# First vectors loaded whole, RWKV's gate applied beside the last two chunks, the rotary key's low part in full-height tiles

## The chip, the cores and the metric

The kernel runs on one core of a Trainium2 chip. The metric is the device time of one execution in microseconds (us). The engines are named as the profile names them: PE (matrix multiplication; PEld is its weight load), DVE (vector), ACT (scalar), POOL (GpSimd) and SP (which issues most of the DMAs).

## What is computed

Two blocks follow each other on one sequence of 512 tokens of width 1024. The first is a two-layer network: layer 0 is an RWKV-7 time mix and a squared-ReLU MLP, layer 1 forgetting attention and an MLP. The second is a gated-DeltaNet mixer beside a latent attention (MLA), and then a layer of 16 experts. All is fp32 in and out. What the three edits touch, cut from the reference:

```python
# modulation of layer 0; sh1 and sc1 are needed first
mod = c_act @ mod_w[0] + mod_b[0]              # 1024 x 6144
sh1, sc1, gt1, sh2, sc2, gt2 = split(mod, 6)
h = rms_norm(x, g) * (1.0 + sc1) + sh1
# RWKV time mix
xx = token_shift(h) - h
xr, xw, xk, xv, xa, xg = (h + xx * mu[j] for j in range(6))
w_log = -softplus(-(w0 + tanh(xw @ w1) @ w2)) - 0.5
a = sigmoid(a0 + (xa @ a1) @ a2)
g = sigmoid(xg @ g1) @ g2                      # 1024 -> 160 -> 1024
... # r, k, v, then the scan over 512 tokens gives y, normalised per head
y = y * ln_w + ln_b + bonus
x = x + (1 + gt1) * ((y * g) @ wo)
# MLA scores: q and k have 128 plain and 64 rotary dimensions, the rotary key is shared by the 8 heads
s = q_nope @ k_nope.T + q_rope @ k_rope.T
```

## The kernel before

Activations lie transposed: eight tiles of 128 channels by 512 tokens. They come from one pool of 58 slots (`self.s()`), in the mixer from a second pool of 23 (also `self.s()`). A large matrix product is made of three products of rounded fp32 parts (fp32r): each operand is split into a high part, made on ACT, and a low part, made on DVE or POOL (`split`, `wsplit`, lines 168 to 206). Small products are plain fp32, and each of those shows in the trace as two passes on PE.

A planner (the Tile framework) orders each engine's instructions at build time, by a priority that grows with the place in the program and by its own estimates of when inputs are ready. On the chip every engine, and the SP queue too, then works strictly in that order. `behind(n)` lowers the priority of what is traced in it by n places. `issue_after(i)` puts what is traced in it behind instruction i on i's engine. A tile whose memory or slot is still in use makes the instruction that would fill it wait, and everything queued behind that.

**The start.** `load_x` (L2438) loads x. `mod_gen` (L319) then makes the two vectors that are needed first, the scale (v = 1) and then the shift (v = 0). Each is c (1 x 1024) times a 1024 x 1024 piece of `mod_w`, loaded as eight chunks of 256 rows by 512 columns into four buffers (`mr`, L327). The products are made in 32 of PE's columns, one row block for each quarter (L341), and then transposed on DVE (L344), summed on PE (L347) and added to the bias (L350). `rwkv` (L515) follows: the norm (`rstd_fm`), t = x times gain times rstd (L525, DVE), h = t + shift (L527, ACT), the token difference d (L529 from t, and its first column from h, L530, both POOL), and the six mixtures h + d mu (`mix`, L538, DVE). The low-rank products come next: w and a (L548, L549, in 64 columns each), then g's 1024 to 160 as one matmul of 128 columns (L560) and one of 32 (L561) for each of eight k. Their weights (`lw`) use the two `wr` buffers of the weight pool, which `rw_wv`'s tiles need next (L178). The value product begins at L271 (`dense_tm`).

**The scan.** Eight chunks of 64 tokens (L902 to L963). A chunk's chain is L920 (state and inputs), L934 (inverse), L945 and L948 (the next state); L952 makes its outputs, and `finish` (L833) normalises two chunks' outputs on DVE and ACT. Beside chunks 4 to 7 run `gates` (g's second product, eight steps) and `boni` (the bonus, eight steps, whose first step of each half fetches four tiles of v). How many steps a chunk gets stands in `GA_` and `GB_`, and they are put 150 places behind. Output tiles 0 and 1 (of 128 tokens) go to DRAM in between (`keep`).

**After the scan.** L969 to L990: the first weights of `rw_wo` are loaded and split on ACT and POOL, tiles 0 and 1 are fetched, and for each of eight channel blocks four 128 x 128 transposes (L985) bring y back to channels by tokens; DVE applies ln_w and the gate (L987), adds the bonus (L988), and the result z is split (ACT, then POOL or DVE). Then the product with `rw_wo` (L1001).

**The MLA scores.** `mla_gen` (L1822) runs between the DeltaNet's steps. Of a head's query rotary part, 64 rows of a tile hold the high part and the other 64 the low part (L1907 to L1909). The rotary key has its high part in both halves. Five matmuls make one 128 x 512 block of scores (L1922 to L1926), of which the last is the query's high part with the key's low part and reads 64 rows only:

```python
nc.tensor.matmul(pS, a[:, dq], kr[0][0], start=False, stop=False)
nc.tensor.matmul(pS, a[q, dq], kr[0][1][q], start=False, stop=True)
```

## Time and profile before

| | us |
|---|---|
| three runs | 2990.75, 2989.43, 2976.11 |
| median | 2989.43 |
| the profiled execution | 2976.45 |
| its span, first to last instruction | 2974.6 |

1.9 us of the profiled execution lie outside its span. The three runs fall on two levels, 2976 and 2990, and the profiled execution is on the lower one.

The page gives busy time by engine over the whole span. The stretches that matter here are 0 to 82 us (the start, to the first value matmul), 395 to 500 us (the scan's second half, and what follows it), 2235 to 2357 us (the MLA scores) and 2440 us to the end (the experts). In the timeline a line is: start, length, engine, line of the kernel, operation, tile written and tile read, shapes, count, and in brackets how long the engine was idle before it and what it waited for. A matmul's length is modelled and overlaps the next one; the step from start to start is the pace.

### The profile page before, as it was taken

To read this page: it belongs to the slowest core of one execution; us is meant where nothing else is said; L and a number is where in the kernel's file an instruction comes from. 1 tells how busy PE (TensorE), PEld (TensorE's weight loads), DVE (VectorE), ACT (ScalarE), POOL (GpSimd) and SP (SyncE) were. 2 spreads that over 40 slices of the span, in tenths; PEclk is the share of its full clock that TensorE was granted. 3 is DMA by queue.
4 is the path that set the end of the run, shared out by engine and by line. 5 is a ranking of instruction groups with operands and counts; after the bars stand their busy time and mean duration, and the time that the engine had idled before them with its cause. 6 is when DMAs were issued, how large, how long until landed. Compare 5 with 4: busy or idle time off the path is not lost.

```text
span 2974.6 us, 38010 instructions
## 1 busy us (share of the span) xinstructions
PE 2771.8 (93%) x15078; PEld 1976.9 (66%) x15078; DVE 1560.9 (52%) x2339; ACT 1057.5 (36%) x1692; POOL 708.1 (24%) x551
## 2 busy tenths in 40 slices
PE   5998888999999999999999997988989998999997
PEld 1665666788876777788886785866867784444333
DVE  4568755555673457565636776628535542212113
ACT  2555433422234467432223452344335432110001
POOL 2446533210110043111112432233252121000000
PEclk9998678999999999999999997999999999999999
DMA  6334215356572321455522322252162377999997
GB/s 211 121 89 143 86 60 177 99 170 198 187 241 78 96 66 45 135 187 194 170 86 71 100 75 76 58 162 57 62 196 91 100 234 293 406 403 409 409 409 299
DMA packets 361010, 502.06 MB, mean 169 GB/s; under 512 B 24768, under 2 KB 236992, under 8 KB 360832
## 3 DMA queue, kind: packets, MB, share of 16 engines
q1 hardware_dynamic: 349600, 479.01, 47.3%
q10 hardware_dynamic: 11232, 20.62, 1.9%
q8 instruction: 119, 1.95, 0.3%
q14 instruction: 59, 0.48, 0.0%
HBM read 471.26 MB, written 26.21 MB: 167 GB/s over the span
## 4 chain that ended last, share of the span: by engine, by line
PE 73%; DVE 13%; DMA 7%; issue 3%; ACT 3%; POOL 1%; SPq 1%; ACTq 0%; DVEq 0%; POOLq 0%
PE psb L243 11%; PE psb L245 11%; PE psb L244 11%; PE psb L2166 6%; PE psf L1322 5%; PE psb L1322 3%; PE psb L2206 3%; DMA rg<-in_w_down_dram 2%; DMA rg<-in_w_up_dram 1%; PE psb L1223 1%; DVE R L1401 1%; DVE s L1491 1%; PE psm L341 1%; PE psm L1957 1%; DVE tm L1399 1%
## 5 line engine op out<-in xcount | busy, mean ns | idle before, releaser
L243 PE MATMUL psb<-s,wh 128*128 128x512 f32 x1384 | 542.9, 393 | 3.1 <-DVE s L987 2.4
L244 PE MATMUL psb<-s,wl 128*128 128x512 f32 x1384 | 540.4, 390 | 0.0
L245 PE MATMUL psb<-s,wh 128*128 128x512 f32 (+1 forms) x1320 | 514.9, 390 | 1.2 <-POOL s L480 0.6
L180 ACT ACTIVATE wh<-wr 128x1024 fp32r<-128x1024 f32 (+1 forms) x221 | 288.2, 1305 | 423.1 <-PE psb L245 250.6
L182 DVE TENSOR_TENSOR wl<-wr,wh 128x1024 fp32r<-128x1024 f32 (+1 forms) x145 | 260.8, 1800 | 261.7 <-ACT wh L180 260.3
L243 PEld LDWEIGHTS psb<-s,wh 128*128 128x128 f32 x1384 | 259.6, 188 | 71.0 <-issue 11.4
L244 PEld LDWEIGHTS psb<-s,wl 128*128 128x128 f32 x1384 | 259.7, 188 | 56.4 <-issue 2.2
L245 PEld LDWEIGHTS psb<-s,wh 128*128 128x128 f32 (+1 forms) x1320 | 247.5, 188 | 57.8 <-issue 2.9
L182 POOL TENSOR_TENSOR wl<-wr,wh 128x1024 fp32r<-128x1024 f32 (+1 forms) x76 | 185.1, 2436 | 411.9 <-ACT wh L180 391.1
L2166 PE MATMUL psb<-rg,s 128*64 128x512 f32 x1024 | 254.8, 599 | 6.3 <-DMA rg<-in_w_up_dram 5.7
L1322 PE MATMUL psf<-f,wh 128*128 128x512 f32 (+1 forms) x688 | 236.6, 416 | 3.0 <-DVE f L1491 2.8
L1018 POOL TENSOR_TENSOR s<-s 128x512 f32<-128x512 f32 x64 | 102.2, 1597 | 514.9 <-ACT s L1016 434.1
L2166 PEld LDWEIGHTS psb<-rg,s 128*64 128x64 f32 x1024 | 83.9, 136 | 148.2 <-issue 125.1
L1322 PEld LDWEIGHTS psf<-f,wh 128*128 128x128 f32 (+1 forms) x688 | 131.8, 195 | 31.0 <-issue 4.5
L1322 PE MATMUL psf<-f,wl 128*128 128x512 f32 (+1 forms) x344 | 142.9, 415 | 3.4 <-POOL wl L182 3.3
L2206 PE MATMUL psb<-rg,s 128*64 128x512 f32 (+1 forms) x544 | 131.8, 573 | 7.4 <-DMA rg<-in_w_down_dram 7.2
L377 DVE SCALAR_TENSOR_TENSOR mt<-mr,crep,mt 128x512 f32<-128x512 f32 x168 | 126.5, 753 | 3.6
L200 ACT ACTIVATE s<-s 128x512 fp32r<-128x512 f32 x112 | 69.7, 625 | 137.4 <-POOL s L1018 73.1
L1322 PE MATMUL psb<-f,wh 128*128 128x512 f32 (+1 forms) x336 | 106.7, 397 | 7.8 <-DVE f L478 5.9
L1025 DVE SCALAR_TENSOR_TENSOR s<-psb,aff,s 128x512 f32<-128x512 f32 x64 | 45.9, 751 | 129.2 <-PE psb L245 129.2
L2206 PEld LDWEIGHTS psb<-rg,s 128*64 128x64 f32 x544 | 45.8, 136 | 80.6 <-issue 58.4
L2214 DVE SCALAR_TENSOR_TENSOR s<-psb,gate,s 128x512 fp32r<-128x512 f32 (+1 forms) x17 | 12.1, 719 | 164.3 <-ACT s L2213 163.9
(579 smaller groups left out, 4895.1 us busy)
## 6 DMA issues: line engine op xcount, KB each, us to landing
rg<-in_w_gate_dram SPq DMA_DIRECT2D x64, 1024.0 KB
rg<-in_w_up_dram SPq DMA_DIRECT2D x64, 1024.0 KB
rg<-in_w_down_dram SPq DMA_DIRECT2D x64, 1024.0 KB
mr<-in_mod_w_dram SPq DMA_DIRECT2D x96, 512.0 KB
wr<-in_mlp_down_dram SPq DMA_DIRECT2D x32, 1024.0 KB
wr<-in_mlp_up_dram SPq DMA_DIRECT2D x31, 1024.0 KB
wr<-in_w_in_dram SPq DMA_DIRECT2D x54, 512.0 KB
mr<-in_w_mod_dram SPq DMA_DIRECT2D x40, 512.0 KB
```

Source lines behind the costliest of these rows:

```text
L180: nc.scalar.activation(hi, raw, AF.Copy)
L182: (lo_eng or self.lo_eng or nc.vector).tensor_tensor(lo, raw, hi.bitcast(F32), op=OP.subtract)
L200: nc.scalar.activation(hi, src, AF.Copy)
L243: nc.tensor.matmul(pt[:mw], hi[k][:, j:j + mw], a, start=(k == 0), stop=False)
L244: nc.tensor.matmul(pt[:mw], lo[k][:, j:j + mw], a, start=False, stop=False)
L245: nc.tensor.matmul(pt[:mw], hi[k][:, j:j + mw], b, start=False, stop=(k == nk - 1))
L377: nc.vector.scalar_tensor_tensor(acc[:, hb], raw[:, d], c, acc[:, hb], op0=OP.mult, op1=OP.add)
L1018: nc.gpsimd.tensor_tensor(sq, r, r, op=OP.mult)
L1025: nc.vector.scalar_tensor_tensor(xT[m], pt, gt[:, m:m + 1], xT[m], op0=OP.mult, op1=OP.add)
L1322: nc.tensor.matmul(pt[:rows, :cols], x, y, start=(k == 0 and q == 0), stop=(k == nk - 1 and q == 2))
L2166: nc.tensor.matmul(B[n][q], XE[hp][k0 // 2][:, o:o + 64], w[e][:, k, n * 512:n * 512 + 512], start=(k0 + k == 0), stop=(k0 + k == 7), skip ...
L2206: last = nc.tensor.matmul(pt[q, :n], HT[(k + i) // 4][:, o:o + 64], w[e][i], start=(k + i == 0), stop=(k + i == 7), skip_group_check=True)
```

## The change

Three edits that do not depend on each other.

1. **Start.** The first two vectors come through a new `mod_first`: the sixteen chunks are 128 rows by all 1024 columns, each in a buffer of its own (16 of 4 KB a partition, in a pool that is closed before `rwkv` opens its own in the same memory). All sixteen loads are traced first. Each chunk gives two matmuls in the same 32 columns, one for each half of the outputs. Between the first vector and the second one's transposes, the norm, all eight t and all eight d (all but its first column) are traced; `issue_after` holds the transposes behind the last t on DVE. The low-rank weights leave the `wr` buffers and share one tile in the pool of `GB`. g's small matmuls go four at a time into four quarters of PE's columns and are summed by one more matmul.
2. **Scan.** The bonus steps are 3, 3, 2, 0 in chunks 4 to 7 where they were 2, 2, 2, 2. A new generator `outs` transposes output tiles 0 to 2 and applies the gate and the bonus to 384 columns, four channel blocks beside chunk 6 and four beside chunk 7, also 150 places behind. After the scan only the last 128 columns are left. The low part of z is made on DVE for four of eight blocks where it was two.
3. **MLA.** The rotary key's low part is kept twice, each in a full tile whose other half is zero, and the fifth matmul reads all 128 rows. One more slot of the 23 is held during the attention.

```diff
-GB_ = (0, 0, 0, 0, 2, 2, 2, 2)
+GB_ = (0, 0, 0, 0, 3, 3, 2, 0)
+MB = 16
...
+    def mod_first(self, jobs, pool):
+        nc = self.nc
+        raws = []
+        for _, W, v, _, _ in jobs:
+            for k in range(KT):
+                raw = pool.tile([128, D], F32, name=self.nm("mw"), tag="mw")
+                nc.sync.dma_start(raw, W[k * 128:k * 128 + 128, v * D:v * D + D])
+                raws.append(raw)
+        after = None
+        for cn, _, _, bias, out in jobs:
+            pts = [self.ps(), self.ps()]
+            for k in range(KT):
+                raw, q = raws.pop(0), slice(32 * (k % 4), 32 * (k % 4) + 32)
+                for hb, pt in enumerate(pts):
+                    nc.tensor.matmul(pt[q], self.crep[cn][:, k], raw[:, hb * 512:hb * 512 + 512], start=(k < 4),
+                                     stop=(k > 3), skip_group_check=True)
+            po = self.bank("m")
+            for hb, pt in enumerate(pts):
+                tp = self.s()
+                with self.tc.issue_after(after) if after else contextlib.nullcontext():
+                    nc.vector.transpose(tp, pt)
+                nc.tensor.matmul(po[:, hb * 16:hb * 16 + 16], self.cst("modsel"), tp[:, 0:512:32], start=(hb == 0),
+                                 stop=(hb == 1), skip_group_check=True)
...
+            after = yield
...
-        wa = self.wp.tile([128, KT, 128], F32, name=self.nm("lw"), tag="wr")
+        lw = gb0.tile([128, 32, 128], F32, name=self.nm("lw"), tag="gb", bufs=1).rearrange("p a b -> p (a b)")
+        wa = lw[:, 0:1024].rearrange("p (k n) -> p k n", n=128)
+        wg = lw[:, 1024:2304].rearrange("p (k n) -> p k n", n=160)
...
-        for k in range(KT):
-            if k % 4 == 0:
-                wg4 = self.wp.tile([128, 4, 160], F32, name=self.nm("lw"), tag="wr")
...
-            xg = mix(5, k)
-            nc.tensor.matmul(pg1, wg[:, 0:128], xg, start=(k == 0), stop=(k == 7))
-            nc.tensor.matmul(pg2[0:32], wg[:, 128:160], xg, start=(k == 0), stop=(k == 7))
+        for kb in (0, 4):
+            xg = [mix(5, kb + j) for j in range(4)]
+            for j in range(4):
+                nc.tensor.matmul(pg1, wg[:, kb + j, 0:128], xg[j], start=(kb + j == 0), stop=(kb + j == 7))
+            for j in range(4):
+                nc.tensor.matmul(pg2[32 * j:32 * j + 32], wg[:, kb + j, 128:160], xg[j], start=(kb == 0), stop=(kb == 4),
+                                 skip_group_check=True)
...
+        nc.scalar.activation(t, pg2, AF.Copy)
+        pg2 = self.ps()
+        nc.tensor.matmul(pg2[0:32], self.cst("modsel")[:, 0:32], t, start=True, stop=True)
...
+            def outs():
+                for g in range(2):
+                    yy = [self.fetch(Y[tt][g]) for tt in range(2)] + [Y[2][g]]
+                    for j in range(4):
+                        fs = slice(j * 128, j * 128 + 128)
+                        pa = self.ps()
+                        for tt in range(3):
+                            nc.tensor.transpose(pa[:, tt * 128:tt * 128 + 128], yy[tt][:, fs], idn)
+                        G, H = (x[:, 0:384] for x in GH[4 * g + j])
+                        nc.vector.scalar_tensor_tensor(G, pa[:, 0:384], self.col("rw_lnw", 4 * g + j), G, op0=OP.mult, op1=OP.mult)
+                        nc.vector.tensor_tensor(G, G, H, op=OP.add)
+                    del yy
+                    yield
...
                         step(GA_[c], GB_[c])
+                        if c > 5:
+                            next(ot2)
...
-            pa = self.ps()
-            for tt in range(4):
-                nc.tensor.transpose(pa[:, tt * 128:tt * 128 + 128], Y[tt][g][:, o:o + 128], idn)
+            if o == 0:
+                pa = self.ps()
+                for j in range(0, 512, 128):
+                    nc.tensor.transpose(pa[:, j:j + 128], Y[3][p // 4][:, j:j + 128], idn)
             G, H = GH[p]
-            nc.vector.scalar_tensor_tensor(G, pa, self.col("rw_lnw", p), G, op0=OP.mult, op1=OP.mult)
-            nc.vector.tensor_tensor(G, G, H, op=OP.add)
-            z.append(self.split(G, lo_eng=nc.gpsimd if p % 4 else nc.vector))
+            v = G[:, 384:512]
+            nc.vector.scalar_tensor_tensor(v, pa[:, o:o + 128], self.col("rw_lnw", p), v, op0=OP.mult, op1=OP.mult)
+            nc.vector.tensor_tensor(v, v, H[:, 384:512], op=OP.add)
+            z.append(self.split(G, lo_eng=nc.gpsimd if p % 2 else nc.vector))
...
-                kr[0] = self.split(kr[0])
+                hi = self.s(F32R)
+                nc.scalar.activation(hi, kr[0], AF.Copy)
+                lows = []
+                for b in (0, 64):
+                    lo = self.s(F32R)
+                    nc.gpsimd.memset(lo[64 - b:128 - b].bitcast(F32), 0.0)
+                    nc.vector.tensor_tensor(lo[b:b + 64], kr[0][b:b + 64], hi[b:b + 64].bitcast(F32), op=OP.subtract)
+                    lows.append(lo)
+                kr[0] = hi, lows
...
-            nc.tensor.matmul(pS, a[q, dq], kr[0][1][q], start=False, stop=True)
+            nc.tensor.matmul(pS, a[:, dq], kr[0][1][h % 2], start=False, stop=True)
...
-            self.run(self.mod_gen(self.mods("c", A["mod_w"][0], m0, (1, 0), M0)))
+            m0m = tc.tile_pool(name="m0", bufs=MB, side="right", reuse_waits="tile")
+            first = self.mod_first(self.mods("c", A["mod_w"][0], m0, (1, 0), M0), m0m.__enter__())
+            next(first)
             G = self.gain(col("norm_mix_g", 0, 8), M0[:, 1])
+            rstd = self.rstd_fm(xT)
+            ts = []
+            for k in range(KT):
+                t = self.s()
+                after = nc.vector.scalar_tensor_tensor(t, xT[k], G[:, k:k + 1], rstd, op0=OP.mult, op1=OP.mult)
+                d = self.s()
+                nc.gpsimd.tensor_tensor(d[:, 1:], t[:, :511], t[:, 1:], op=OP.subtract)
+                ts.append((t, d))
+                xT[k] = None
+            first.send(after.ins)
+            m0m.__exit__(None, None, None)
```

## Rows read from the trace of the kernel before

**Rows 1.** The page, part 1: PE's busy time, share of the span, instructions.

```profile
PE 2771.8 (93%) x15078; PEld 1976.9 (66%) x15078; DVE 1560.9 (52%) x2339; ACT 1057.5 (36%) x1692; POOL 708.1 (24%) x551
```

**Rows 2.** DMA view of 0 to 60 us: GB/s in forty slices of 1.5 us.

```profile
GB/s 0 174 409 397 400 393 377 378 397 388 277 53 294 388 395 384 360 352 344 242 123 356 337 326 323 307 286 200 238 249 354 382 180 49 15 0 0 11 0 0
```

**Rows 3.** Timeline of the start, PE: g's first products, the first value matmul.

```profile
64.39 1.13 PE L560 MATMUL psb<-s,lw 128*128 128x512 f32 x2
...
66.42 1.12 PE L560 MATMUL psb<-s,lw 128*128 128x512 f32 x2
...
81.99 0.51 PE L271 MATMUL psb<-wh,s 128*128 128x512 f32 x1 [1.28 <-ACT s L200]
```

**Rows 4.** Timeline of the start, DVE.

```profile
40.59 0.72 DVE L344 STREAM_TRANSPOSE mt<-psm 128x512 f32<-128x512 f32 x1 [8.23 <-PE psm L341]
41.82 0.69 DVE L350 TENSOR_TENSOR M<-psm,P 32x8 f32<-32x8 f32 x4 [0.51 <-PE psm L347]
42.54 6.29 DVE L525 SCALAR_TENSOR_TENSOR s<-s,gain,s 128x512 f32<-128x512 f32 x7
48.75 19.89 DVE L538 SCALAR_TENSOR_TENSOR s<-s,P,s 128x512 f32<-128x512 f32 x24
...
78.11 2.73 DVE L538 SCALAR_TENSOR_TENSOR s<-s,P,s 128x512 f32<-128x512 f32 x4
```

**Rows 5.** Groups of 0 to 82 us by form, ACT and POOL: h and d.

```profile
L529 POOL TENSOR_TENSOR s<-s 128x511 f32<-128x511 f32 x8 | 11.7, 1465 | 16.1 <-DVE s L525 16.1
L527 ACT ACTIVATE s<-s,M 128x512 f32<-128x512 f32 x8 | 5.5, 722 | 22.1 <-DVE M L350 20.6 <-DVE s L525 1.4
L530 POOL TENSOR_SCALAR s<-s 128x1 f32<-128x1 f32 x8 | 5.2, 647 | 13.7 <-ACT s L527 13.7
```

**Rows 6.** Timeline at 2462 us, PE: four column quarters, two matmuls in each.

```profile
2462.41 1.08 PE L2009 MATMUL psb<-s,s 128*32 128x512 f32 x8
2463.29 1.06 PE L2010 MATMUL psb<-s,s 128*32 128x512 f32 x8
```

**Rows 7.** Stretches of the scan's end: length, busy times, PEclk, DMA share, GB/s.

```profile
434.20:455.10 20.90, 19.53 (x179) 12.71 (x178) 7.28 (x13) 5.07 (x9) 8.94 (x9) 0.67 0.24 73
425.70:434.20 8.50, 8.50 (x151) 6.64 (x150) 3.15 (x6) 2.37 (x4) 2.08 (x3) 1.00 0.03 5
```

**Rows 8.** Timeline after the scan, PE: transposes, first matmul of rw_wo.

```profile
476.16 5.81 PE L985 MATMUL psb<-C,s 128*128 128x128 f32 x28 [4.98 <-DMA s<-kd]
...
486.86 0.77 PE L243 MATMUL psb<-s,wh 128*128 128x512 f32 x1 [2.36 <-DVE s L987]
```

**Rows 9.** Timeline of the SP queue, scan's end (merged: a length holds its waits).

```profile
433.17 18.24 SPq L1265 DMA_DIRECT2D s<-kd  x4
```

**Rows 10.** Groups of 470 to 500 us: DVE's two steps for z, POOL's weight split.

```profile
L988 DVE TENSOR_TENSOR s<-s,s 128x512 f32<-128x512 f32 x8 | 9.6, 1225 | 0.0
...
L182 POOL TENSOR_TENSOR wl<-wr,wh 128x1024 fp32r<-128x1024 f32 (+1 forms) x2 | 6.9, 3442 | 16.9 <-ACT wh L180 16.9
...
L987 DVE SCALAR_TENSOR_TENSOR s<-psb,P,s 128x512 f32<-128x512 f32 x8 | 5.7, 738 | 0.9 <-PE psb L985 0.9
```

**Rows 11.** Timeline of one MLA unit, PE.

```profile
2258.23 0.40 PE L1924 MATMUL psf<-f,f 128*128 128x512 f32 x1
2258.46 0.40 PE L1925 MATMUL psf<-f,f 128*128 128x512 f32 x1
2258.79 0.50 PE L1926 MATMUL psf<-f,f 64*128 64x512 f32 x1
2259.21 0.66 PE L1949 MATMUL psf<-C,f 128*128 128x128 f32 x4
```

**Rows 12.** Stretches from the MLA scores to the experts, columns as in rows 7.

```profile
2260.00:2280.00 20.00, 20.00 (x117) 15.27 (x116) 9.88 (x23) 9.06 (x20) 5.14 (x4) 1.00 0.23 76
...
2440.00:2460.00 20.00, 20.00 (x90) 16.57 (x89) 6.68 (x7) 6.66 (x8) 0.00 (x0) 1.00 0.26 85
...
2500.00:2600.00 100.00, 99.73 (x506) 46.07 (x504) 15.71 (x28) 17.41 (x30) 0.00 (x0) 1.00 1.01 399
```

More of the change, by code (lines that the diff above doesn't have):

```diff
@@ L351, in mod_gen @@
             yield
+    def mod_first(self, jobs, pool):
[21 more added lines that the diff above has]
+                                 stop=(hb == 1), skip_group_check=True)
+            for a in range(4):
+                q = slice(32 * a, 32 * a + 32)
+                nc.vector.tensor_tensor(out[q], po[q, a:32:4], bias[q], op=OP.add)
+            after = yield
     def mod_vgen(self, jobs):
@@ L512, in mod_pgen, with rwkv @@
         yield
-    def rwkv(self, x_dram, G, sh, gt, xT):
+    def rwkv(self, x_dram, G, sh, gt, ts):
         nc, tc, A = self.nc, self.tc, self.A
@@ L520, in rwkv @@
         self.open_weights(1024)
-        rstd = self.rstd_fm(xT)
         hT, xx = [], []
         for k in range(KT):
-            t = self.s()
-            nc.vector.scalar_tensor_tensor(t, xT[k], G[:, k:k + 1], rstd, op0=OP.mult, op1=OP.mult)
+            t, d = ts.pop(0)
             h = self.s()
             nc.scalar.activation(h, t, AF.Identity, bias=sh[:, k:k + 1])
-            d = self.s()
-            nc.gpsimd.tensor_tensor(d[:, 1:], t[:, :511], t[:, 1:], op=OP.subtract)
             nc.gpsimd.tensor_scalar(d[:, 0:1], h[:, 0:1], -1.0, None, op0=OP.mult)
@@ L532, in rwkv @@
             xx.append(d)
-            xT[k] = None
-        del rstd, t, h, d
+        del t, h, d
         def mix(j, k):
@@ L887, in boni @@
                         yield
+            def outs():
[11 more added lines that the diff above has]
+                    yield
             self.run(prepare(0))
-            gt8, bn8 = gates(), boni()
+            gt8, bn8, ot2 = gates(), boni(), outs()
             step = lambda n, m: [next(z, None) for z in [gt8] * n + [bn8] * m]
@@ L976, in rwkv @@
                                    [128, KT, b - a], lo_eng=nc.gpsimd))
[L977 to L979 removed]
         z = []
         for p in range(8):
[L982 to L985 removed]
+            o = (p % 4) * 128
+            if o == 0:
+                pa = self.ps()
+                for j in range(0, 512, 128):
+                    nc.tensor.transpose(pa[:, j:j + 128], Y[3][p // 4][:, j:j + 128], idn)
             G, H = GH[p]
[L987 to L989 removed]
+            v = G[:, 384:512]
+            nc.vector.scalar_tensor_tensor(v, pa[:, o:o + 128], self.col("rw_lnw", p), v, op0=OP.mult, op1=OP.mult)
+            nc.vector.tensor_tensor(v, v, H[:, 384:512], op=OP.add)
+            z.append(self.split(G, lo_eng=nc.gpsimd if p % 2 else nc.vector))
             GH[p] = None
@@ L1909, in load @@
                 nc.gpsimd.tensor_tensor(a[q[1]], r[q[0]], a[q[0]].bitcast(F32), op=OP.subtract)
-                QK[h] = self.split(self.fetch(Qd[h]), lo_eng=nc.gpsimd) + (a, q[0]) + self.split(Kt[h], lo_eng=nc.vector)
+                QK[h] = self.split(self.fetch(Qd[h]), lo_eng=nc.gpsimd) + (a,) + self.split(Kt[h], lo_eng=nc.vector)
                 Kt[h] = None
@@ L1918, in score @@
                 load(h + 1)
-            qh, ql, a, q, kh, kl = QK[h]
+            qh, ql, a, kh, kl = QK[h]
             dq = slice(qt * 128, qt * 128 + 128)
```

14 lines of the change are left out of this document (6 added, 8 removed).

## The prediction

> **What bounds the kernel now.** I read the page first: PE is busy for 93% of the span [rows 1], so an edit pays where it shortens PE's own stream, or a stretch in which PE stands. There are three such stretches here, and each is read by another view. The DMA slices show the start: in most slices ahead of 39 us the queues move 300 to 409 GB/s [rows 2], so loading sets the pace of the first 40 us, with two holes (53 and 123 GB/s) that loading into four buffers leaves. DVE's timeline shows what follows: the transpose of the products (L344) waits 8.23 us for them, and seven of the eight t start only behind it, at 42.54 us, because DVE works in order [rows 4]. The next fence on PE is g's small products, whose eight steps of 2.03 us end far behind DVE (DVE's 24 mixtures end at 68.64 us, the value product starts at 81.99) [rows 3, 4]. For the scan's end the stretches and the timeline are read: chunk 5 takes 8.5 us, chunk 6 20.9 [rows 7], and behind the scan PE waits 4.98 us for a DMA and then starts `rw_wo` at 486.86 [rows 8]. In the MLA stretch PE is busy all the time (20.00 of 20 us) [rows 12], and one of its matmuls has a step of its own [rows 11]. After 2500 us the experts' weights come at 399 GB/s with a DMA share of 1.01 [rows 12]: that part is bound by loading.
>
> **The start, step by step.** *Loads.* The slices before 39 us add up to 12.3 MB (their sum, 8174 GB/s, times 1.5 us). 0.8 MB of these are the low-rank weights (256, 256 and 320 KB by their shapes), which now come behind the sixteen chunks; 11.4 MB remain. The eight slices from the third on average 392 GB/s, and the start costs 2.3 us (the first two slices). So the last chunk lands at 2.3 + 11.4/0.392 = 31.5 us, some 0.5 later for its landing. *Products.* The two matmuls of a chunk lie in the same quarter of PE's columns and follow each other: a quarter takes 0.87 us for one matmul, and four quarters run side by side [rows 6]. One chunk costs 1.74 us, less than the four-chunk spacing, so PE isn't the bound, and the last product ends at 33.7 us where it ended just ahead of the transpose at 40.59. The transposes (0.72), the sum and the bias end at 42.51 now, 1.9 us after the products [rows 4]; there are two transposes at the end instead of one, so 2.3: the shift is there at 36.0, 6.5 us earlier. If nothing of the load moved, this term is 0; 8 is its other end.
>
> Here a rule speaks against the sum. The slices run at 377 to 409 GB/s. The Trainium skill (DMA: Bandwidth & Descriptors, "Where 436 GB/s comes from") says that transfers from HBM bind at about 358 GB/s for one core. By that, the chunks would land at 34.2 us and the edit would gain 2.7 us less; this trace shows more than 358 over twelve microseconds, so I keep 392.
>
> *t and d.* The seven t (6.29 us on DVE) and the eight d (11.7 us on POOL) stand behind the shift today [rows 4, 5]; they now lie beside the second vector's loading, which lasts about 10 us from the first vector to the second. After the shift only one h (0.72) and one column of d (0.65) are left [rows 5], 1.4 us instead of 6.2 (42.54 to 48.75). The first mixture comes at about 37.5 us where it came at 48.75: 11.2 us in all. *Mixtures.* Beside POOL's d they take 0.83 us each (19.89/24), without it 0.68 (2.73/4) [rows 4]; 16 of them end at about 49, and the products of w and a 1 us later, at 50, where g's products started at 64.39: 14.4 us. *g.* Today eight times 2.03 us [rows 3]. Then eight full matmuls at 0.87 and two sets of four quarters at 0.87, with some 0.2 for each change of shape: 9.3 us. A sum over the quarters is added (one matmul, 0.9, and ACT's copy, 0.6); it hides if ACT works on the value's inputs meanwhile, and costs up to 2.5 if ACT's order puts it first. First value matmul at 60.5 to 63 instead of 81.99. The products of v, k and r that follow are PE's own stream, and PE is the engine at 93% [rows 1], so I take what is won here to move everything behind it. The low-rank weights are the cover that can go: their tile lies over the chunks' memory, so they can be issued as late as 34 us. They are needed at 38, and PE has slack against DVE's 0.68 a mixture, so I put no cost on it; 8 us is what it costs if they land at 46. **Sum for the start: -20 us, between -12 and -24.**
>
> **The scan, step by step.** What leaves the path behind the scan is three quarters of z's work: DVE's eight gates of 0.738 and eight additions of 1.225 us (slower than a gate, though they read as much) [rows 10] become 128-column ones, and 24 of 32 transposes go. `rw_wo` starts 10.7 us after the first transpose [rows 8]. With only the last tile left, a first z needs four transposes, a gate, an addition and a split: about 3 us. DVE's part for the other columns, eight times (0.60 + 0.55) = 9 us (my estimate, three quarters of 0.74 and 0.68 with a fixed part), has room beside chunks 6 and 7, where it is busy 7.28 of 20.9 us [rows 7]. That is -7.5, with -11 as its end. On the other side are 24 transposes in a scan in which PE is busy 19.53 of 20.9 us. In chunk 6 the steps put beside it already cost 12.4 us (20.9 against 8.5), also as the clock fell to 1.2 GHz for much of it (mean share 0.67) [rows 7]. The transposes are 150 places behind and fit the 4.98 us in which PE waits today [rows 8], so I charge 0.5; a second such stretch, less a part of the gain, would be +8. SP's queue moves too: four fetches of y stand ahead of `rw_wo`'s weights instead of behind. The fetches of v took 18.24 us for four, most of it waiting for slots [rows 9].
>
> The additions beside POOL's two weight splits (3.4 us each) average 1.225 us where the split between them is 0.738 for the gate from PSUM [rows 10]. The Trainium skill (GPSIMD Engine Reference, "Specifications") says that POOL's memory interface is shared with VectorE and that DVE instructions with two SBUF inputs contend. By it the last additions stay slow whatever their length, and the scan's term would be nearer -5; I leave it inside the bounds. **Sum for the scan: -7 us, between +8 and -11.**
>
> **MLA.** From L1925 to L1926 the step is 0.33 us, from there to the next matmul 0.42; between two full matmuls of 512 columns it is 0.23 [rows 11]. So the 64-row matmul costs 0.75 where 0.46 is due: 0.29 us, 32 times, 9.3 us, on an engine without a gap [rows 12]. The two zero fills and the halves of the low part are done once, on POOL and DVE. One slot fewer of 23 can delay a head's load by a few units; I leave 3 us for that. **Sum: -9 us, between -6 and -10.**
>
> **Total.** 2976.45 - 20 - 7 - 9 = 2940.5 for an execution like the profiled one. The median of the three runs lies 13.0 us higher, and which level the next runs fall on isn't known; I add half: 2947.
>
> **Rivals.** *(a) The start gains half.* The low-rank weights or the ACT order hold the first products to about 46 us: -10 instead of -20, 2957. For it: they queue behind 8 MB, in rows of 256 bytes, and the hole of 53 GB/s is where one of them ran [rows 2]. Against: 8 us of slack before they are due. *(b) The scan pays.* +8 instead of -7: 2962. For it: chunk 6. Against: PE's idle stretch behind the scan. *(c) The experts absorb it.* If the weight stream from 2500 us on [rows 12] started by its own clock, nothing would be left: 2976 to 2990, no change. For it: a share of 1.01. Against: at 2440 to 2460 us the share is 0.26 [rows 12], so the ring is full and waits for PE; the stream starts when PE does. *(d) Slower.* The fetches of y wait for slots as those of v do (18.24 us [rows 9]), the scan's PE stream stands at their transposes, and the rest of the scan then runs at the lower clock (12.4 us as in chunk 6). Twice 18.2 plus 12.4 is +49 in place of -7: 2947 + 56 = 3003. It decides from the point at which the first of these transposes stands ahead of chunk 7's L920 in PE's order.
>
> **How the numbers follow.** Forecast 0.58, (a) 0.14, (b) 0.10, (c) 0.10, (d) 0.08. Range: the best ends add up to -45, 2931 on the lower level, less 2 us for scatter; the worst to -10, 2966 there and 2979 on the upper. 2929 to 2979 holds the forecast, (a), (b) and part of (c). A measurement of this kernel tells about 0.5%, 15 us, from no change: forecast, (a) and (b) are faster by more, 0.82; (c) is within, 0.10; (d) slower, 0.08.
>
> **What would show it.** Right: the first mixture near 37.5 us and the first value matmul at 60 to 63; DVE's eight t in one row ahead of the second vector's transposes; `rw_wo`'s first matmul less than 10 us behind the last L952; no step over 0.24 us around the fifth score matmul; the stretch between `rw_wo` and the MLA as long as now. Wrong: PE's w and a products waiting for a DMA; chunk 7 longer than 15 us; the experts starting no earlier than now.

## The result, and the profile after

Five runs of the changed kernel took 2950.97, 2964.71, 2965.78, 2965.85 and 2966.23 us, median 2965.8; the kernel before had 2989.0 beside them. The ratio is 0.9936, with an interval of 0.9913 to 0.9958: 23 us less where 42 were forecast against the median. A second comparison (e5_all, below) gave 0.9948 (0.9924 to 0.9972), medians 2963.8 and 2976.7, so 13 us. The direction was right, the size was not. The profiled execution took 2965.78 us (span 2964.0), 10.7 below that of before; for that comparison the forecast was 2940.5, 36 below.

The starts of the same matmuls in both traces make a ledger (us from the start of the span):

| | before | after | gained so far |
|---|---|---|---|
| first value matmul | 81.99 | 70.82 | 11.2 |
| chunk 5 of the scan begins | 425.70 | 416.80 | 8.9 |
| last output matmul of the scan ends | 470.05 | 459.91 | 10.1 |
| first matmul of `rw_wo` | 486.86 | 478.00 | 8.9 |
| first matmul behind `rw_wo` | 536.20 | 533.17 | 3.0 |
| first MLA score | 2237.19 | 2236.95 | 0.2 |
| last MLA unit begins | 2344.12 | 2333.81 | 10.3 |
| first expert matmul | 2490.99 | 2480.84 | 10.2 |
| span | 2974.6 | 2964.0 | 10.6 |

So the start gave 11 (20 forecast), of which 9 were left at the scan's chunk 5; the scan took 6 (7 of gain forecast), the MLA gave 10 (9 forecast). Between 536 and 2237 us no edit lies, and there the ledger loses 2.8: 1.4 of it is the difference of two larger amounts (the DeltaNet, below), the other 1.4 stay unexplained.

In the changed kernel's line numbers the t are L2428, d L2430, a vector's transposes L376 and bias L381, the mixtures L564, the gate and bonus on 384 columns L933 and L934 (transposes L931), those of the last tile L1037 and L1038 (transposes L1034), `finish`'s last step L880, the weight split L184, `rw_wo`'s matmuls L245 to L247, a score's five matmuls L1980 to L1984.

The timeline of the start, with DVE, POOL, PE and ACT; the rows of before are [rows 3 to 5]:

```profile
25.10 1.49 DVE L447 TENSOR_TENSOR s<-s,s 128x512 f32<-128x512 f32 x2
28.67 1.98 PE L450 MATMUL psb<-s,C 128*128 128x512 f32 x4
30.59 3.67 PE L370 MATMUL psb<-mw,crep 128*32 128x512 f32 x30
31.41 0.63 ACT L461 ACTIVATE s<-s 128x512 f32<-128x512 f32 x1
32.07 10.07 DVE L2428 SCALAR_TENSOR_TENSOR s<-s,gain,s 128x512 f32<-128x512 f32 x8 [5.49 <-ACT s L461]
32.91 5.81 POOL L2430 TENSOR_TENSOR s<-s 128x511 f32<-128x511 f32 x4 [20.74 <-DVE s L2428]
38.76 5.29 POOL L2430 TENSOR_TENSOR s<-s 128x511 f32<-128x511 f32 x4
44.20 0.69 DVE L381 TENSOR_TENSOR M<-psm,P 32x8 f32<-32x8 f32 x4 [0.70 <-PE psm L377]
45.97 10.69 DVE L564 SCALAR_TENSOR_TENSOR s<-s,P,s 128x512 f32<-128x512 f32 x16 [1.09 <-POOL s L557]
58.51 3.70 PE L587 MATMUL psb<-s,lw 128*128 128x512 f32 x8 [0.73 <-DVE s L564]
66.77 1.07 PE L589 MATMUL psb<-s,lw 128*32 128x512 f32 x8
69.66 0.59 ACT L597 ACTIVATE s<-psb 32x512 f32<-32x512 f32 x1 [1.14 <-PE psb L596]
70.16 4.25 ACT L202 ACTIVATE s<-s 128x512 fp32r<-128x512 f32 x8
70.82 0.50 PE L273 MATMUL psb<-wh,s 128*128 128x512 f32 x1 [1.20 <-ACT s L202]
```

The second vector's products end at 34.26 us, but its transposes stand on DVE behind the eight t, which begin at 32.07, when the norm's last step (L461) is done, and take 10.07 us beside POOL's d. The first mixture comes at 45.97.

The end of the scan: DVE, POOL, PE and the SP queue. Before it was [rows 7 to 10]:

```profile
444.57 15.75 SPq L180 DMA_DIRECT2D wr<-in_rw_wo_dram  x2
460.42 1.00 SPq L1315 DMA_DIRECT2D s<-kd  x2
459.84 1.08 PE L931 MATMUL psf<-C,s 128*128 128x128 f32 x6
464.32 0.61 DVE L933 SCALAR_TENSOR_TENSOR s<-psf,P,s 128x384 f32<-128x384 f32 x1
466.16 6.85 POOL L184 TENSOR_TENSOR wl<-wr,wh 128x1024 fp32r<-128x1024 f32 x2 [16.22 <-ACT wh L182]
466.45 2.20 DVE L1038 TENSOR_TENSOR s<-s,s 128x128 f32<-128x128 f32 x1
468.58 4.98 DVE L880 TENSOR_TENSOR s<-s,st 128x512 f32<-128x512 f32 x1
473.70 1.09 PE L1034 MATMUL psb<-C,s 128*128 128x128 f32 x4 [7.81 <-DVE s L880]
478.00 0.77 PE L245 MATMUL psb<-s,wh 128*128 128x512 f32 x1
489.38 0.82 PE L931 MATMUL psf<-C,s 128*128 128x128 f32 x6
490.58 1.07 PE L931 MATMUL psf<-C,s 128*128 128x128 f32 x6 [0.38 <-DVE s L933]
```

No gate ran beside the chunks: the first is at 464.32, 4.4 us behind the scan's end (459.9). Two of y's fetches stand in SP's queue behind `rw_wo`'s weights; the second load of these waits 14.9 us, until the scan's last output matmul is done. Two additions on DVE, due 0.28 and 0.69 us by their fellows, last 2.20 and 4.98 beside POOL's split. Twelve transposes lie in the middle of `rw_wo`'s product.

One MLA unit on PE. The fifth matmul (L1984) now has a step of 0.23 before it and behind it, where it had 0.33 and 0.42 [rows 11]:

```profile
2248.12 0.39 PE L1983 MATMUL psf<-f,f 128*128 128x512 f32 x1
2248.35 0.39 PE L1984 MATMUL psf<-f,f 128*128 128x512 f32 x1
2248.58 0.60 PE L2007 MATMUL psf<-C,f 128*128 128x128 f32 x4
```

**The DeltaNet, where nothing was edited.** Its two triangular inverses each end in small matmuls (the inverse's tail). From an inverse's first 32 x 32 matmul to the first state update behind it the traces show two lengths only: 31.7 to 33.5 us, or 43.2 to 45.1 (two kernels with added work, e13_fill and e15_before_fill, lie at 33 to 47). In the profile of before the first inverse is long and the second short (45.1, 31.7); in that of after it is the other way (33.5, 44.7). These are the stretches, columns as in [rows 7]; first before, then after:

```profile
1835.00:1850.00 15.00, 15.00 (x219) 10.46 (x219) 2.74 (x4) 2.37 (x4) 0.52 (x1) 0.50 0.12 34
```

```profile
1835.00:1850.00 15.00, 15.00 (x369) 12.67 (x369) 5.68 (x9) 7.25 (x12) 5.38 (x5) 1.00 0.08 20
2080.00:2090.00 10.00, 10.00 (x105) 7.26 (x103) 2.06 (x3) 3.37 (x6) 3.38 (x2) 0.50 0.26 78
2090.00:2100.00 10.00, 10.00 (x134) 8.89 (x130) 2.73 (x4) 2.26 (x4) 0.94 (x1) 0.50 0.02 4
```

PE is busy in all of them; the granted clock is 1.2 GHz (0.50) in the long ones. So the two profiled executions hold one long inverse each and can be compared; by themselves the inverses moved the ledger by 11.6 us one way and 13.0 back.

### The profile page after: what moved, and what is told of

The parts are those of the page before. It is cut to its first block, busy times and chain, and to the rows that moved or that the text cites. A ratio compares the mean times of both kernels' runs of the same rounds, so it can differ in the third digit from the quotient of the medians.

```text
span 2964.0 us, 38037 instructions
## 1 busy us (share of the span) xinstructions
PE 2760.2 (93%) x15084; PEld 1985.8 (67%) x15084; DVE 1560.2 (53%) x2358; ACT 1056.9 (36%) x1693; POOL 699.7 (24%) x551
## 5 line engine op out<-in xcount | busy, mean ns | idle before, releaser
L245 PE MATMUL psb<-s,wh 128*128 128x512 f32 x1384 | 542.9, 393 | 1.6 <-ACT s L202 0.9
L247 PE MATMUL psb<-s,wh 128*128 128x512 f32 (+1 forms) x1320 | 515.4, 391 | 1.8 <-POOL s L511 0.6
L184 DVE TENSOR_TENSOR wl<-wr,wh 128x1024 fp32r<-128x1024 f32 (+1 forms) x145 | 258.8, 1786 | 262.4 <-ACT wh L182 262.2
L245 PEld LDWEIGHTS psb<-s,wh 128*128 128x128 f32 x1384 | 259.6, 188 | 70.0 <-issue 11.4
L246 PEld LDWEIGHTS psb<-s,wl 128*128 128x128 f32 x1384 | 259.5, 188 | 56.6 <-issue 2.2
L247 PEld LDWEIGHTS psb<-s,wh 128*128 128x128 f32 (+1 forms) x1320 | 247.1, 187 | 60.4 <-issue 2.9
L184 POOL TENSOR_TENSOR wl<-wr,wh 128x1024 fp32r<-128x1024 f32 (+1 forms) x76 | 184.5, 2429 | 417.5 <-ACT wh L182 397.9
```

The costliest lines, as they stand in the source:

```text
L184: (lo_eng or self.lo_eng or nc.vector).tensor_tensor(lo, raw, hi.bitcast(F32), op=OP.subtract)
L245: nc.tensor.matmul(pt[:mw], hi[k][:, j:j + mw], a, start=(k == 0), stop=False)
L246: nc.tensor.matmul(pt[:mw], lo[k][:, j:j + mw], a, start=False, stop=False)
L247: nc.tensor.matmul(pt[:mw], hi[k][:, j:j + mw], b, start=False, stop=(k == nk - 1))
```

## The experiments

e1 to e4 ran on one chip beside the same runs of the kernel before; so did e5 to e8, e9 to e12 and e13 to e16, each on another chip. Since the times of every kernel are scattered over two dozen us, the stage lengths of the profiles are the sharper tool; all lengths are differences of starts in the traces, in us. "V" is the first value matmul, "gap" the time from the scan's last output matmul's start to `rw_wo`'s first, "wo" from there to the first matmul behind `rw_wo`, "inv" the two inverses, "MLA" from the first score to the last unit.

| | V | gap | wo | inv 1, 2 | MLA | ratio to before, interval |
|---|---|---|---|---|---|---|
| before | 82.0 | 17.0 | 49.3 | 45.1, 31.7 | 106.9 | 1 |
| after | 70.8 | 18.3 | 55.2 | 33.5, 44.7 | 96.9 | 0.9936, 0.9913 to 0.9958 |
| e1_start | 72.3 | 17.1 | 49.4 | 45.0, 43.2 | 106.9 | 0.9992, 0.9969 to 1.0014 |
| e2_scan | 84.0 | 18.3 | 55.2 | 33.5, 44.7 | 106.9 | 1.0046, 1.0023 to 1.0070 |
| e3_mla | 79.3 | 17.2 | 49.4 | 45.1, 44.8 | 96.9 | 0.9986, 0.9958 to 1.0015 |
| e4_no_scan | 72.5 | 17.2 | 49.4 | 32.0, 43.2 | 96.9 | 0.9946, 0.9921 to 0.9970 |
| e5_all | 71.2 | 18.3 | 55.2 | 33.5, 44.6 | 96.9 | 0.9948, 0.9924 to 0.9972 |
| e6_norm_first | 64.4 | 18.3 | 55.1 | 33.4, 33.2 | 96.9 | 0.9913, 0.9880 to 0.9946 |
| e7_split_dve | 72.6 | 15.0 | 56.8 | 33.5, 33.2 | 96.8 | 0.9912, 0.9882 to 0.9942 |
| e8_d_late | 74.2 | 18.3 | 55.1 | 32.0, 31.7 | 96.9 | 0.9919, 0.9888 to 0.9950 |
| e9_no_scan_fix | 63.9 | 14.9 | 49.7 | 45.0, 44.7 | 96.8 | 0.9926, 0.9899 to 0.9953 |
| e10_all_fix | 63.9 | 15.0 | 56.6 | 45.1, 44.6 | 96.8 | 0.9919, 0.9892 to 0.9945 |
| e11_outs_first | 63.8 | 18.0 | 50.9 | 45.0, 44.6 | 96.9 | 0.9927, 0.9891 to 0.9963 |
| e12_before_dve | 82.4 | 15.3 | 49.7 | 33.5, 44.7 | 106.9 | 1.0019, 1.0001 to 1.0036 |
| e13_fill | 64.1 | 15.4 | 49.7 | 35.6, 34.5 | 96.9 | 0.9949, 0.9924 to 0.9973 |
| e14_outs_early | 64.4 | 11.7 | 54.3 | 33.5, 33.1 | 96.9 | 0.9906, 0.9878 to 0.9935 |
| e15_before_fill | 80.2 | 17.1 | 49.4 | 32.8, 47.2 | 106.9 | 1.0066, 1.0040 to 1.0092 |
| e16_no_scan_fix | 64.2 | 15.0 | 49.7 | 45.0, 33.2 | 97.1 | 0.9891, 0.9855 to 0.9927 |

V scatters by itself: 79.3 to 84.0 in the five profiles with the old start (mean 81.6), 70.8 to 72.6 in the five with the new one as it is (mean 71.9). Gap and "wo" together repeat within 0.6 us wherever that part of the kernel is the same.

### The three edits apart

e1_start, e2_scan and e3_mla each put one of the three edits into the kernel before; their heads are:

```diff
-            self.run(self.mod_gen(self.mods("c", A["mod_w"][0], m0, (1, 0), M0)))
+            first = self.mod_first(self.mods("c", A["mod_w"][0], m0, (1, 0), M0), m0m.__enter__())
```

```diff
-            gt8, bn8 = gates(), boni()
+            gt8, bn8, ot2 = gates(), boni(), outs()
```

```diff
-            nc.tensor.matmul(pS, a[q, dq], kr[0][1][q], start=False, stop=True)
+            nc.tensor.matmul(pS, a[:, dq], kr[0][1][h % 2], start=False, stop=True)
```

e4_no_scan is the changed kernel with the second of these undone, e5_all the changed kernel itself.

> The kernel before with the start's edit alone. Theory A (the two traces are read as a ledger, stage by stage): the first value matmul at about 71 us, as with all three edits (82 before), the scan's chunk 4 about 9 us earlier than before, nothing else moved; 9 to 11 us below the kernel before on the same level. Theory B (the prediction's -20 is right for the start, and something in the other two edits hides it): first value matmul at 62, time 20 us lower.

> The kernel before with the scan's edit alone. Theory A: the end of the product with rw_wo comes 5 to 6 us later against the scan's start than before (24 transposes are in PE's stream of rw_wo or beside it, and an addition on DVE stands for 4 us behind POOL's weight split); 5 to 6 us above the kernel before. Theory B (the scan gains the 7 us forecast, and the loss seen with all three is the clock's): 7 us below before.

> The kernel before with the MLA edit alone. All theories: 32 steps shorter by 0.3 us, the stretch of the scores 9 to 10 us shorter, time 9 to 10 us lower. Theory C (the executions' two levels depend on where the slow-clock stretch of the DeltaNet's inverses falls, and any shift of the program's times can move it): the difference of single executions can be off by 12 us either way, and the trace shows which of the two inverses runs at a granted clock of 0.5.

> The changed kernel with the scan's edit undone (start and MLA stay). Theory A: 5 to 6 us below the changed kernel on the same level, so about 19 to 21 below the kernel before. Theory B: 7 us above the changed kernel.

> The changed kernel itself once more, beside the kernel before on one chip. If the single edits add up (start -9, scan +6, MLA -10 by the ledger of the traces), 12 to 13 us below the kernel before when like is compared with like; if the 23 us of the first comparison hold, 23. The trace shows which of the DeltaNet's two inverses runs its end at a granted clock of 0.5 (expected: about 12 us in the time for each that does, and none of it an effect of an edit).

By stages theory A holds to 1.5 us throughout: V at 72, gap and `rw_wo` together 73.5 against 66.4, the scores 10.1 shorter. By whole times it is blurred, and the single edits do not add up: medians of -3, +12 and -1 us, where all three together give -13 (e5_all). e1_start shows no gain at all (0.9992, its interval holds 1), and e3_mla shortens the scores by 10.1 us, yet its ten runs (2953.8 to 2981.6) average little below the kernel before; the profiles of both have both inverses long, where that of before has one. Whether an edit changes how often an inverse is long, and with it the mean time, was not tested. e4_no_scan against e5_all were run beside different chips' runs of before; their ratios agree within their intervals, and only the stages show the 7 us.

The 31 runs of the kernel before beside e1 to e4 fall into three groups: 5 at 2963.0 to 2966.2, 21 at 2970.1 to 2980.0, 5 at 2982.2 to 2987.4 (the upper border is drawn by eye), about 11 us apart, as no, one or two long inverses would have it. Their mean granted clocks go the same way: 0.958 to 0.961, 0.954 to 0.958, 0.952 to 0.954. That the unprofiled runs are made so is argued; the profiles show it for one execution of each kernel. Four of the five runs of before in the first comparison lay at 2985 to 2991, the upper group. By that reading about half of the 23 us of the first comparison is which group was drawn.

### The start

```diff
+            rstd = self.rstd_fm(xT)
             first = self.mod_first(self.mods("c", A["mod_w"][0], m0, (1, 0), M0), m0m.__enter__())
             next(first)
             G = self.gain(col("norm_mix_g", 0, 8), M0[:, 1])
-            rstd = self.rstd_fm(xT)
```

> The changed kernel with the norm traced ahead of the first vector's products. Theory D (the eight t begin late, at 32.07 us, because the norm's two additions on DVE and its eight matmuls on PE stand behind the first vector in their engines' order): the t begin at 25 us, when the gain is there, end at 35 to 36, the first mixture at 39 to 40 (45.97 in the changed kernel), the first value matmul at 64 to 65 (70.82); 6 to 7 us off. Theory E (the second vector's loading ends late, and the t were not what held it): the first mixture stays within 2 us of 45.97.

DVE and PE in its timeline:

```profile
25.60 10.08 DVE L2428 SCALAR_TENSOR_TENSOR s<-s,gain,s 128x512 f32<-128x512 f32 x8
35.71 1.31 DVE L376 STREAM_TRANSPOSE s<-psb 128x512 f32<-128x512 f32 x2
39.50 10.69 DVE L564 SCALAR_TENSOR_TENSOR s<-s,P,s 128x512 f32<-128x512 f32 x16 [1.09 <-POOL s L557]
64.35 0.50 PE L273 MATMUL psb<-wh,s 128*128 128x512 f32 x1 [1.20 <-ACT s L202]
```

Theory D holds with its numbers: 25.60, 39.50, 64.35; 6.5 us gained by the order of tracing alone. The t still last 1.26 us each. The next kernel asks why:

```diff
-                d = self.s()
-                nc.gpsimd.tensor_tensor(d[:, 1:], t[:, :511], t[:, 1:], op=OP.subtract)
...
             nc.scalar.activation(h, t, AF.Identity, bias=sh[:, k:k + 1])
+            nc.gpsimd.tensor_tensor(d[:, 1:], h[:, :511], h[:, 1:], op=OP.subtract)
```

> The changed kernel with the difference d made from h, behind the second vector, instead of from t ahead of it. Theory F for the start (DVE's t last 1.52 us instead of 0.75 because POOL's d run beside them): the eight t take 5.4 us instead of 10.1 and end at 37.5, the second vector's transposes begin there (42.18 in the changed kernel); the mixtures then run beside the d and are slowed in their turn, so that the first value matmul gains little or nothing. Theory H (t slow for another reason, such as the loads): the t stay at 1.5 us.

DVE in its timeline, the t and the sixteen mixtures:

```profile
33.66 5.39 DVE L2429 SCALAR_TENSOR_TENSOR s<-s,gain,s 128x512 f32<-128x512 f32 x8 [6.96 <-ACT s L461]
43.87 16.14 DVE L565 SCALAR_TENSOR_TENSOR s<-s,P,s 128x512 f32<-128x512 f32 x16 [2.08 <-POOL s L558]
```

The t by themselves, least, median and greatest duration in ns, first in the changed kernel, then here:

```profile
L2428 DVE SCALAR_TENSOR_TENSOR s<-s,gain,s x8: 745/1520/1527, 32.1 to 40.6; 128x512 f32<-128x512 f32 x8
```

```profile
L2429 DVE SCALAR_TENSOR_TENSOR s<-s,gain,s x8: 747/750/753, 33.7 to 38.3; 128x512 f32<-128x512 f32 x8
```

Without POOL's d beside them all eight are at 0.75 us, where six of eight were at 1.52, and the sixteen mixtures, now beside the d, take 16.14 instead of 10.69. Theory F holds: the price goes to whatever runs on DVE beside POOL's d. V came 3.4 us later (74.2), but 1.6 of these had passed before the first t (33.66 against 32.07).

### The scan

```diff
             pre.append(self.wsplit([(slice(0, b - a), A["rw_wo"][:, a:b].rearrange("(k p) n -> p k n", p=128))],
-                                   [128, KT, b - a], lo_eng=nc.gpsimd))
+                                   [128, KT, b - a], lo_eng=nc.vector))
```

e7_split_dve has this in the changed kernel, e12_before_dve in the kernel before.

> The changed kernel with the low parts of rw_wo's first two weight tiles made on DVE instead of POOL. Theory F (an addition on DVE with two operands in SBUF that begins beside POOL's split lasts until that ends: 2.20 us where 0.28 is due and 4.98 where 0.69 is due): both additions at their due length, 6 us off DVE's row, 3.5 us of splits put on; first matmul of rw_wo 2 to 3 us nearer to the scan's end than the 18.2 us of the changed kernel. Theory G (the additions are long because they wait for something else): they stay long, and the first matmul comes 3 us later.

> The kernel before with rw_wo's first two low parts made on DVE instead of POOL, nothing else. If a DVE addition beside POOL's split lasts until that ends, L846 (2.41 us) and L988 (1.225 mean of eight) fall to 0.7 us, 5 to 6 us in all, against 3.5 us of splits put on DVE: rw_wo's first matmul 1 to 3 us nearer to the scan's end (17.0 in the kernel before). If they are long for another reason, 3 us further.

DVE in the timeline of e7_split_dve, then two groups of 470 to 500 us in e12_before_dve:

```profile
464.81 1.23 DVE L184 TENSOR_TENSOR wl<-wr,wh 128x1024 fp32r<-128x1024 f32 x1
466.28 0.68 DVE L880 TENSOR_TENSOR s<-s,st 128x512 f32<-128x512 f32 x1
466.88 0.29 DVE L1038 TENSOR_TENSOR s<-s,s 128x128 f32<-128x128 f32 x1
```

```profile
L988 DVE TENSOR_TENSOR s<-s,s 128x512 f32<-128x512 f32 x8 | 6.8, 884 | 0.0
...
L846 DVE TENSOR_TENSOR s<-s,st 128x512 f32<-128x512 f32 x2 | 1.4, 688 | 0.0
```

Both fell to their due length once POOL was idle, and the gap lost 3.4 and 1.7 us. L988 keeps 0.884 us, since four of z's low parts are still POOL's. In the changed kernel 1.6 of the 3.4 come back in `rw_wo` (56.8). In whole times e12_before_dve is no faster than before (1.0019; its profile has one long inverse, as that of before, but seven of its ten runs lie at 2987 to 2991); the stages alone show its 1.3 us.

Then the transposes in `rw_wo`'s product. With norm first and the low parts on DVE, e10_all_fix has all three edits, e9_no_scan_fix leaves the scan's out; e11_outs_first also holds the last tile's transposes behind the others, and e14_outs_early brings the bonus, the steps of `gates` and the fetches forward:

```diff
+                with tc.issue_after(lastout):
                     for j in range(0, 512, 128):
                         nc.tensor.transpose(pa[:, j:j + 128], Y[3][p // 4][:, j:j + 128], idn)
```

```diff
-GA_ = (0, 0, 0, 0, 2, 2, 1, 0)
-GB_ = (0, 0, 0, 0, 3, 3, 2, 0)
+GA_ = (0, 0, 0, 0, 3, 2, 0, 0)
+GB_ = (0, 0, 0, 0, 4, 4, 0, 0)
...
+                fy = [[self.fetch(Y[tt][g]) for tt in range(2)] for g in range(2)]
```

> The changed kernel without the scan's edit, with the norm ahead of the first vector's products and with rw_wo's first two low parts made on DVE. Start as with the norm first (first value matmul 64 to 65), MLA as changed, scan as before but the POOL-DVE collision taken away. If the ledger adds up: 9 + 6 to 7 + 10 + 0 to 3, so 25 to 29 us below the kernel before, 6 us below the changed kernel with the norm first.

> All three edits, with the norm first and the low parts on DVE. If the 24 transposes beside and in rw_wo's product are what the scan's edit costs, this stays 3 to 4 us above the same kernel without the scan's edit, because the time from rw_wo's first matmul to its end stays near 55 us where it was 49. If the collision with POOL was all that it cost, this is level with it or below.

> As the kernel with all three edits and both mends, but the last tile's transposes are held behind the 24 others on PE, so that none of these stands in rw_wo's product. If the 5.8 us by which that product became longer are the transposes and the late z, it is back near 49 to 50 us, and its first matmul comes later (20 to 22 us behind the scan's end instead of 15 to 16); the sum of both tells what the edit can bring at best: 0 to 2 us below the kernel without this hold. If the product stays at 55 us, something else slows it.

> All three edits, norm first, low parts on DVE; the bonus steps traced at chunks 4 and 5 (4 and 4) and the four fetches of y traced together ahead of rw_wo's weights, so that in PE's order all 24 transposes stand ahead of the last tile's. If the place behind the scan is what the edit costs: the first gate on 384 columns runs ahead of the scan's end (4.6 us behind it in the changed kernel), rw_wo's product is back at 49 to 50 us, and scan and product together are below those without the edit. If it is DVE's own work (8 times 0.61 and 0.55 added to 8 times 0.35 and 0.28), the time from the scan's end to rw_wo's end stays at 68 to 72 us, or chunks 5 to 7 take longer by what is won.

DVE and PE in the timeline of e14_outs_early, where the scan ends at 453.3:

```profile
452.15 0.61 DVE L935 SCALAR_TENSOR_TENSOR s<-psf,P,s 128x384 f32<-128x384 f32 x1
464.81 0.79 PE L245 MATMUL psb<-s,wh 128*128 128x512 f32 x1 [1.92 <-ACT s L202]
477.15 0.82 PE L933 MATMUL psf<-C,s 128*128 128x128 f32 x6
```

Gap and `rw_wo` together are 64.6 us without the scan's edit, 71.6 with it (7 us, where 3 to 4 were expected; the whole times of the two cannot be told apart), 68.9 with the last tile's transposes held back, 66.0 with bonus and fetches forward; 66.4 in the kernel before and 73.5 in the changed one. In e11_outs_first `rw_wo` is back at 50.9, so the transposes and the late z were what lengthened it. In e14_outs_early the first gate runs 1.2 us ahead of the scan's end, and chunks 4 to 7 take 1.2 us less than without the edit, so that it comes out level (113.2 against 113.0 us from chunk 4's first output matmul to the end of `rw_wo`; 118.1 with the edit as it was). So place and fetches cost 5 to 6 us of it. But seven of the eight gates still run behind the scan and nine transposes inside `rw_wo` (54.3, where 49 to 50 were expected): what the edit would bring with all gates beside the chunks is not shown.

### The inverses

```diff
+        pf = self.ps()
+        pv = P.rearrange("p a b -> p (a b)")
+        for k in range(14):
+            nc.tensor.matmul(pf, self.cst("ident"), pv[:, 0:512], start=(k == 0), stop=(k == 13))
```

> The changed kernel without the scan's edit, with the norm first, the low parts on DVE, and 14 matmuls added (their sums are read by nothing) ahead of each of the DeltaNet's two inverses, 12.2 us of PE's time each, where PE stands 10.9 us today. Theory K (the tail of an inverse falls to a granted clock of 0.5 because PE stood before it): both tails at 32 to 33.5 us, the times of the runs in one cluster, their spread well under 12 us; against the same kernel without the 14 matmuls up to 24 us less in runs where both tails were slow, 1 to 3 us more where neither was. Theory L (chance, or the tail's own small matmuls): tails of 32 or 44 us as before, times spread over 12 to 24 us, 1 to 3 us more in the mean.

> The kernel before with the 14 matmuls ahead of each inverse and nothing else. Theory K: both tails at 32 to 33.5 us and times near the lowest cluster of the kernel before (2961 to 2966) plus 1 to 3 us, without the clusters 12 and 24 us above. Theory L: the same three clusters as the kernel before, 1 to 3 us higher.

> The changed kernel without the scan's edit, with the norm first and the low parts on DVE, once more, as the base of the first of these: 23 to 27 us below the kernel before where like is compared with like, in clusters 12 us apart.

PE in the timeline of e15_before_fill, the added matmuls and the tail's first:

```profile
1776.34 12.25 PE L1399 MATMUL psb<-P,C 128*128 128x512 f32 x28 [2.24 <-DVE P L1394]
1818.44 0.32 PE L1419 MATMUL psb<-T,UB 32*32 32x32 f32 x4 [9.73 <-DVE T L1411]
```

The test missed its mark: the added work ran 30 us ahead, and PE still stood 9.7 us at the same place (9.4 in e13_fill). Ahead of the second tail it stood 6.7 and 6.8 us instead of 11.8, and one of these two was long (47.2), the other short (34.5). Theory K is neither shown nor refuted; the fill cost 20 us by whole times in the kernel before (1.0066) and about 16 in the other (0.9949 against 0.9891), where 1 to 3 were expected. e16_no_scan_fix is the same kernel as e9_no_scan_fix. Their eight runs lie at 2936.9 to 2963.4. With 0.9926 and 0.9891 it is the version that I would keep: by stages 6.6 us at V and 8.9 us at gap and `rw_wo` below the changed kernel, with 1.2 given back in chunks 4 to 7. Its interval still overlaps that of the changed kernel.

## Why the prediction was wrong, step by step

**Loads and products: right.** 33.7 us was forecast for the last product, 34.26 came. The load slices of the changed kernel (0 to 60 us, forty of 1.5) have no hole where before had two [rows 2]:

```profile
GB/s 0 169 414 400 403 386 397 418 410 404 415 404 412 418 396 418 410 404 415 404 392 385 269 228 309 348 225 288 388 384 328 4 0 11 5 0 0 0 0 272
```

At 385 to 418 GB/s the 358 of the rule weighed there did not bind. The Trainium skill says as much elsewhere (Perfetto Trace Analysis, "Roofline": the figure is a core's share when its neighbour loads too).

**t and d: the step that failed at the start.** The prediction laid eight t and eight d "beside the second vector's loading" and counted them as free. That needed the t to begin with the gain at 25.2 us. They began at 32.07, since the norm's additions and sums were traced behind the first vector and stood behind it on DVE and PE (e6_norm_first moves them: 25.60). The prediction's own row has 0.90 us a t (6.29 for seven), by which eight would have ended ahead of the products; they took 1.26 on average, because DVE and POOL then ran in lock step (e8_d_late: 0.67). The transposes, held behind the last t, came at 42.2 instead of 34. That is nearly the whole miss: first mixture 45.97 instead of 37.5, 8.5 us late, of which e6_norm_first wins 6.5 back (39.50). From there the forecast's lengths held: 12.5 us from the first mixture to g's first matmul (12.5 forecast), 9.3 for g (9.3), and 3.0 to the first value matmul, where 2.5 had been named as the cost if ACT put the sum of the quarters first, as it did (69.66 ahead of 70.16).

So rival (a), that the start gains half, came in its size (11 us, first product of w and a at 46.77), but not by its cause: the low-rank weights did not hold that product. Its row puts PE's wait down to a DMA, which is one of the signs named for a wrong prediction; yet it starts 0.05 us behind the end of the first mixture (46.72), and in e6_norm_first, where that mixture ends at 40.25, it follows as closely. The two rows, the changed kernel first:

```profile
46.77 1.12 PE L577 MATMUL psb<-s,lw 128*64 128x512 f32 x1 [2.62 <-DMA mr<-in_mod_w_dram]
40.30 1.12 PE L577 MATMUL psb<-s,lw 128*64 128x512 f32 x1 [2.62 <-DVE s L564]
```

**The scan: the sign was wrong.** Rival (b) came, with 6 us instead of 8, but not by chunk 6, whose length hardly moved (20.9 to 21.3 us in this profile; 23.0 in e5_all). The failed sentence is that DVE's part "has room beside chunks 6 and 7". The room was there by busy share; the order had none: on PE the transposes stood behind the bonus, whose last transposes ended at 458.5 us, and those of the last four blocks needed the two fetches that waited for the scan's end. The prediction had all four fetches ahead of `rw_wo`'s weights. All eight gates therefore ran behind the scan, each split into two instructions of 0.61 and 0.35 us where one of 0.74 had been, and the same for the additions: more work on the path, not less. That the order is the reason is shown in part: e14_outs_early, with bonus and fetches forward, wins 5 to 6 us back, but brings only one gate ahead of the scan's end. The charge of 0.5 for the transposes became 3.0 us of PE's time from 478 us on, and 3.5 us in which PE stood ahead of them until a gate was done (3.1 of it just ahead of `rw_wo`'s first matmul), in PE's groups of 478 to 533 us:

```profile
L931 PE MATMUL psf<-C,s 128*128 128x128 f32 x15 | 3.0, 311 | 3.5 <-DVE s L933 3.5
```

Rival (d) did not come.

**POOL beside DVE: mis-sized.** The prediction put 2 us on this and kept it inside the bounds. It took 1.9 + 4.3 us from DVE's row behind the scan. The single durations behind [rows 10] show it already before (least, median and greatest in ns): the mean of 1.225 us is made of additions of 0.68 and of a few very long ones.

```profile
L988 DVE TENSOR_TENSOR s<-s,s x8: 677/982/2735, 479.8 to 493.1; 128x512 f32<-128x512 f32 x8
```

The reading of the mixtures has the same fault: 0.83 us is the mean pace of five that last 1.52 beside a d and of nineteen that last 0.74.

**MLA: right.** 10.1 for 9; the slot that is held cost nothing that shows.

**The experts: right, rival (c) fell.** They begin 10.2 us earlier and end 10.6 earlier.

**The level.** The median of 2989 against which the forecast stood lies in the upper of three groups, and half of the distance was added for it. This alone moves a median by about 12 us, as much as the whole change does; that the medians came 23 us apart, and not 11 to 13, is by the reading above luck of the draw. Between the two profiled executions, with one long inverse in each, 36 us were forecast and 10.7 came: 9 to 11 are missing at the start, 13 at the scan.

## What to carry to other kernels

A step moved under a load is free only from the moment its last input is there: trace the whole chain of that input (here the norm), and look at what stands ahead of it on each engine. Room by busy share is not room in order: before work is moved beside a loop, find in the trace which instruction would stand ahead of it, on each engine and in the DMA queue. And pair DVE's two-input instructions with POOL's only where DVE has time to lose.

## What the runs showed of the hardware

**DVE beside POOL.** A DVE instruction with two operands in SBUF that starts while POOL's two-input subtraction runs ends shortly behind that one's end (0.55 us with 512 columns, 0.15 in the one case with 128): t lasts 1.52 us instead of 0.75, `finish`'s addition 4.98 instead of 0.69. POOL pays too: a d takes 1.48 us beside the t and 1.03 for the last one, which has no t beside it. Beside POOL's step on a single column (L530) DVE keeps its 0.74, and so does a gate that reads PSUM and one SBUF tile beside POOL's split. The Trainium skill (SBUF — State Buffer, "Who interferes with whom") has this as an exclusive lock held for the whole instruction; the traces agree. The other page of the Trainium skill, which the prediction quoted, names the contention and gives no size for it; 2 us were too few here.

**The clock of a busy PE.** The tail of an inverse ran 11 to 13 us longer at a granted clock of 0.50 with PE busy all the time, in 8 of the 12 tails of the first six kernels profiled (before, after, e1 to e4). PE stands 10.8 to 10.9 us ahead of the first inverse's tail and 11.8 ahead of the second's in the profiles of before and after, where one of each is long and the other short, so that pause alone does not decide it. Nor does the kernel: e9_no_scan_fix and e16_no_scan_fix are the same, and their second tails took 44.7 and 33.2 us. What does stays open.
